# A hybrid decoder step on one core: the sixth tile pair by seven products, four operand sums and four low parts made by GpSimd

## The chip, the core and the metric

The kernel runs on one core of a Trainium2 chip. The core's engines work side by side, each through its own queue: PE (TensorE, the matmuls), DVE (VectorE), ACT (ScalarE), POOL (GpSimd) and SP, which issues DMAs. The metric is the device time of one execution in microseconds. The profile of one execution adds where each engine was busy and what it waited for.

## The reference

One inference step of a one-layer decoder trunk for 512 prompt positions and 8 x 4 sample positions, 544 in all, with a model width of 1024 and an inner width of 4096. A mixer (a recurrent branch and windowed attention) comes first. The change lies in the second half, the convolutional feed-forward block:

```python
def _conv_ffn(h, prev, w_up, conv_w, conv_b, w_down):
    u = h @ w_up                                        # (544, 1024) @ (1024, 8192)
    u, conv_state = _causal_dwconv(u, prev, conv_w, conv_b)   # width 3
    val, gate = jnp.split(u, 2, axis=-1)
    return (jax.nn.gelu(gate, approximate=True) * val) @ w_down, conv_state
```

with `h` the RMS norm of the mixer's output `x`, and the result normed and added to `x`. All of it is in float32.

## The kernel before

**Split matmuls.** Each operand of a matmul is held as a high part (rounded by a copy to a narrower format, on ACT) and a low part (operand minus high part, on DVE). A product is the sum of three matmuls per block of 128 rows: high x high, high x low, low x high. `product` writes one product as 4 blocks x 3 = 12 matmuls with 272 columns; the low part of the weight is read by the third of each three.

**Tile pairs.** The 8192 columns of `w_up` are 64 tiles of 128. Tile p (a value) and tile 32 + p (its gate) form pair p. The 1024 rows of a tile are two halves, and the 544 positions are two halves of 272, so a plain tile takes four products, a plain pair eight. The seven-product form (in the manner of Strassen) treats the pair as a 2 x 2 matrix of weight blocks and the operand as another, and takes seven products, named a11, a12, p2, p3, p1, p4 and a22. It needs four sums of operand blocks (t1, t2, t3, t4, made once, each as two 128x544 tiles with high and low part), and for each pair sums of weight blocks.

**Operands.** `norm_chain(1)` norms the second half of the positions (`h2t`, called `second`), makes the operands b12 and b22 of the plain products, and then, step by step, the sums t2, t3, t1 and t4 from `first` (the tiles `h2f`) and `second`, their high parts (`high`) and low parts (`low`). It is a generator: each `yield x` gives the order back for x ticks, and each product advances the time by half a tick (`slot` calls `round_`). So the place of its instructions among the products is written out by hand. On PE, ACT and DVE instructions run in the order in which the program gives them; POOL's and SP's are ordered by the scheduler of the language.

**The order of products.** Pairs 0 to 3 (`early`) run their first halves while the second half of the positions is still being normed, and then 16 products of their second halves. After these comes the list `plan`: pairs below `PLAIN` as eight plain products (kind "q"), the others by seven (kind "s"), with down halves (kind "dn": 12 matmuls with 256 or 288 columns, one half of the positions of one of eight column tiles of `w_down`, for a group of four pairs) put in behind the products named in `places`. Four down halves go with pairs 4 and 5 together, since the first group is ready only after 12 products of the plan: before, the order is tile 4, tile 36, tile 5 (four products each), three down halves, tile 37, one down half, and then pair 6.

**Weights.** `units` lists the weight halves in the order of their use; a plain unit serves two products, a seven-product unit one. `consumed` counts units, and `ahead` works a fixed number of units ahead of the products: `load` (a DMA of 512 KB into one of five buffers, `raw_up`), `do_high` (ACT, four units ahead), `do_low` (DVE, three ahead), and, for seven-product pairs, `sums`, four and three units ahead of the pair's p2: p3's weight as a sum on DVE into a tile of its own, p1's in place on DVE, and p2's and p4's by two DMAs that add into a second copy of the value tile (`raw_up_s`, a third load of the pair). These two DMAs are issued by POOL, the second after the first has landed.

**Evacuation.** Results of plain products go from PSUM to the tile `u` by copies on ACT (`plain_done`). Results of the seven products are combined: copies `e` on ACT, and additions or subtractions on DVE (`pair`). Then DVE applies the convolution's taps (`tap`), ACT the gelu (`glu` stage 0), DVE the product z (stage 1), and ACT and DVE split z for the down product (stages 2 and 3, fH and fL).

Of the kernel before, what the change touches and what calls it, by code (L numbers as in the profile page):

```python
# [11 lines left out]
F32 = mybir.dt.float32  # L12
F32R = mybir.dt.float32r
AF = mybir.ActivationFunctionType
ALU = mybir.AluOpType
AX = mybir.AxisListType

P = 128
# [40 lines left out]
HP = 150  # L59
NSTART = (1, 0.5)  # L60
EARLY = 4
PLAIN = 6
FB = (0.5,)
LASTS = 6
HELD = 5
TY = 1
TX = 4
DNS = 5
LAST_PLACES = {29: ('p3', 'p1', 'a22'), 30: ('p3', 'p1', 'a22'), 31: ('p1', 'a22')}
FIRST = 5  # L70
ATTN = (8, 10, 12, 14, 16, 18, 20, 22, 24, 26, 29, 32, 35, 38, 40, 42)
SAMPLE = (41, 46)
# [49 lines left out]
def hawk_step(ctx, tc, I, O):  # L122
    nc = tc.nc
    act, dve, pool, pe = nc.scalar, nc.vector, nc.gpsimd, nc.tensor
# [16 lines left out]
    def S(name, dt=F32):  # L141
        return sp.tile([P, SLOT], dt, tag="s", name=name)

    def T(name, dt=F32):
        return tp.tile([P, FLAT + 4], dt, tag="t", name=name)
# [13 lines left out]
    def f32(ap):  # L159
        return ap.bitcast(F32)  # L160
# [4 lines left out]
    def sub(out, a, b):  # L165
        dve.tensor_tensor(out=out, in0=a, in1=b, op=ALU.subtract)  # L166
# [4 lines left out]
    def add(out, a, b):  # L171
        dve.tensor_tensor(out=out, in0=a, in1=b, op=ALU.add)  # L172
# [984 lines left out]
    def total(accs, n, nm):  # L1157

        ps = PX("pst_" + nm)
        for z, acc in enumerate(accs):  # L1160
            mm(ps[:, :n], ones, acc[:, :n], z == 0, z == len(accs) - 1)
        return ps

    def root_table(ps, n, nm):

        y, w = (T(f"{x}_{nm}")[:, :n] for x in ("ry", "rw"))
        act.activation(y, ps[:, :n], AF.Abs_reciprocal_sqrt, scale=1.0 / D, bias=epst)
        act.activation(w, y, AF.Square, scale=1.0 / 32.0)
        return y, w
# [30 lines left out]
    def part_pool(which):  # L1200

        if not parts:
            trans.close()
            parts["e"] = ctx.enter_context(tc.tile_pool(name="parts", bufs=E_BUFS))
            parts["p"] = ctx.enter_context(tc.tile_pool(name="psums", bufs=2))
        return parts[which]
# [6 lines left out]
    def operand(nm, k, j):  # L1213

        if (nm, k // 2) not in B:
            B[nm, k // 2] = [S(f"{nm}{x}{k // 2}", F32R) for x in "HL"]
        return B[nm, k // 2][j][:, (k % 2) * HN:(k % 2 + 1) * HN]

    def operand2(nm, k2, j):

        operand(nm, 2 * k2, j)
        return B[nm, k2][j][:, 0:2 * HN]
# [9 lines left out]
    def norm_chain(a, acc):  # L1232
        lo, hi = HALF2[a]
        n = hi - lo
        with tc.high_priority(offset=HP):
            ps = total([acc], n, f"m{a}")
        yield YS[a]
        with tc.high_priority(offset=HP):
            yw = root_table(ps, n, f"m{a}")
            if a:  # L1240
                yield 0.5
            rep = root_newton(ps, n, *yw)
            acc2 = T(f"accx{a}")
            sq = {}

            def x1_(c):
                return x1[c][:, lo:hi]

            for c in range(0 if a else 8):
                m_ = mt[c][:, lo:hi]  # L1250
                stt(m_, m_, pvn[:, G_POST + c:G_POST + c + 1], rep[:, :n], ALU.mult, ALU.mult)
                pool.tensor_tensor(out=x1_(c), in0=x1_(c), in1=m_, op=ALU.add)
                sq_sum(acc2, x1_(c), n, c == 0, f"x{a}_{c}")
            for g in range(6 if a else 0):
                for c in range(2 * g, 2 * g + 2) if g < 4 else ():
                    m_ = mt[c][:, lo:hi]
                    stt(m_, m_, pvn[:, G_POST + c:G_POST + c + 1], rep[:, :n], ALU.mult, ALU.mult)
                    pool.tensor_tensor(out=x1_(c), in0=x1_(c), in1=m_, op=ALU.add)
                for c in range(2 * g - 3, 2 * g - 1) if 1 <= g < 6 else ():
                    if 0 <= c < 8:  # L1260
                        sq[c] = acc2 if c == 0 else T(f"sq_x{a}_{c}")
                        act.activation(sq[c][:, :n], x1_(c), AF.Square)
                for c in ((), (), (), (), (1, 2, 3), (4, 5, 6, 7))[g]:
                    add(acc2[:, :n], acc2[:, :n], sq[c][:, :n])
                yield 0.5
        yield NORM_TICKS[a]
        with tc.high_priority(offset=HP):
            ps = total([acc2], n, f"f{a}")
        yield YS[a]
        with tc.high_priority(offset=HP):  # L1270
            yw = root_table(ps, n, f"f{a}")
            if a:
                yield 0.5
            rep = root_newton(ps, n, *yw)

            def normed(c, dst):
                stt(dst, x1[c][:, lo:hi], pvn[:, G_FPRE + c:G_FPRE + c + 1], rep[:, :n], ALU.mult, ALU.mult)

            def first(k2):
                return h2f[k2][:, 0:2 * HN]  # L1280

            if a == 0:
                for k2 in range(5):
                    if k2 < 4:
                        for c in (2 * k2, 2 * k2 + 1):
                            normed(c, h2_half0(c))
                        act.activation(operand2(("b11", "b21")[k2 // 2], k2 % 2, 0), first(k2), AF.Copy)
                    if k2:
                        o = [operand2(("b11", "b21")[(k2 - 1) // 2], (k2 - 1) % 2, j) for j in range(2)]
                        sub(o[1], first(k2 - 1), f32(o[0]))  # L1290
                return
            n2 = {}

            def second(k2):
                return n2[k2]

            def high(nm, src):
                for k in range(2):
                    act.activation(operand2(nm, k, 0), src(k), AF.Copy)

            def low(nm, src):
                for k in range(2):
                    sub(operand2(nm, k, 1), src(k), f32(operand2(nm, k, 0)))

            for k2 in range(5):
                if k2 < 4:
                    n2[k2] = npool.tile([P, 2 * HN], F32, name=f"h2t{k2}")
                    for z in range(2):
                        normed(2 * k2 + z, n2[k2][:, z * HN:(z + 1) * HN])
                    act.activation(operand2(("b12", "b22")[k2 // 2], k2 % 2, 0), n2[k2], AF.Copy)  # L1310
                if k2:
                    o = [operand2(("b12", "b22")[(k2 - 1) // 2], (k2 - 1) % 2, j) for j in range(2)]
                    sub(o[1], n2[k2 - 1], f32(o[0]))
                if k2 in (2, 4):
                    yield 0.5
            for c in range(8):
                nc.sync.dma_start(out=x1d[c], in_=x1[c][:, 0:NT])
            t2 = [T(f"t2_{k}")[:, 0:2 * HN] for k in range(2)]
            for k in range(2):
                sub(first(k), first(k), second(k))  # L1320
                stt(t2[k], first(k), -1.0, second(2 + k), ALU.mult, ALU.subtract)
                yield 0.5
            for k in range(2):
                add(first(2 + k), first(2 + k), t2[k])
                yield 0.5
            high("t2", lambda k: t2[k])
            yield 0.5
            low("t2", lambda k: t2[k])
            yield 0.5
            for k in range(2):  # L1330
                sub(second(k), second(k), second(2 + k))
                yield 0.5
            yield TX
            for nm, src in (("t3", second), ("t1", first), ("t4", lambda k: first(2 + k))):
                high(nm, src)
                yield TY
                low(nm, src)
                yield TY

    def out_done(c, acc):  # L1340
# [36 lines left out]
    for p_ in range(EARLY, 32):  # L1377
        if p_ < PLAIN:
            todo_ = [("q", j, u, a) for j in (p_, 32 + p_) for u in range(2) for a in range(2)]
            places = [x for x in todo_ if x[2] == x[3] == 1]  # L1380
        else:
            todo_ = [("s", p_, nm) for nm in (XOF if p_ < 31 else ENDS)]
            places = [x for x in todo_ if x[2] in LAST_PLACES.get(p_, ("a12", "p3", "p1", "a22"))]
        for x in todo_:
# [15 lines left out]
    raws, usplit, used = {}, {}, [0, 0, 0]  # L1400
# [56 lines left out]
    def sums(p_, part):  # L1457
        w = {nm: source(("s", p_, nm)) for nm in ("p1", "p2", "p4", "a22")}
        if part == 0:
            raws["p3", p_] = part_pool("p").tile([P, 4, P], F32, tag="p", name=f"p3_{p_}")  # L1460
            add(raws["p3", p_], w["p2"], w["p1"])
        else:
            add(w["p1"], w["p1"], w["a22"])
            pool.dma_start(out=w["p2"], in_=w["p1"], accum_op=ALU.add)
            pool.dma_start(out=w["p4"], in_=w["p2"], accum_op=ALU.add)  # L1465
# [532 lines left out]
```

## Time and profile before

| what | value |
| --- | --- |
| median of 3 runs | 974.34 us (974.23 to 974.61) |
| the profiled execution | 973.95 us |
| its span in the profile | 972.2 us |
| matmuls on PE | 7634 |
| DVE, ACT, POOL busy | 756.3, 553.9, 167.9 us |

The span runs from the first to the last instruction of the profile; the execution's own time has 1.75 us around it. "Busy" counts the time in which an engine works on an instruction. A row of a timeline gives start, length, engine, line, operation, output <- inputs, shape, and in brackets the idle time of the engine ahead of it and what ended that. A low part of a weight is written `wl_...`, a high part `wh_...`; `pq` is the PSUM tile of plain products, `pux`, `puy`, `puz` those of the seven-product form, `pmdn` that of the down halves.

### The profile page before, as it was taken

The numbers are of one execution on the slowest core, as the hardware profiler recorded it, in microseconds if no ns is written. First come the engines' busy times: TensorE is split into PE (matmuls) and PEld (weight loads), VectorE is DVE, ScalarE is ACT, GpSimd is POOL, SyncE is SP. The second block draws the span as 40 slices with busy tenths as digits, with TensorE's granted clock in tenths as the row PEclk, the third lists the DMA queues.
The fourth block names the chain that finished last, engine by engine and source line by source line (L and its number), as shares of the span: only waits on it lengthen the run. The fifth ranks groups of instructions, "written<-read, shape, count | busy, mean of one in ns | idle before, by whom it ended". The sixth has DMA issues, their size and how long they took to land.

```text
span 972.2 us, 20023 instructions
## 1 busy us (share of the span) xinstructions
PE 963.0 (99%) x7634; PEld 955.2 (98%) x7634; DVE 756.3 (78%) x1599; ACT 553.9 (57%) x1349; POOL 167.9 (17%) x282
## 2 busy tenths in 40 slices
PE   9999999999999999999999999999999999999997
PEld 8999999999999999999999999999999999999996
DVE  5777888857858555599967888787888888888875
ACT  6544443467476425566767665655555555656653
POOL 2242000003406330230010111111011101020024
PEclk9999999999999999999999999999999999999999
DMA  7775535532334547135157575857576766668612
GB/s 229 236 213 180 151 89 147 162 93 87 108 110 128 179 115 189 52 121 186 45 117 182 128 198 123 192 130 181 136 181 157 171 155 156 170 145 219 201 31 92
DMA packets 234203, 143.07 MB, mean 147 GB/s; under 512 B 25012, under 2 KB 218940, under 8 KB 234076
## 3 DMA queue, kind: packets, MB, share of 16 engines
q1 hardware_dynamic: 224300, 120.21, 41.8%
q0 software_dynamic: 9696, 19.42, 11.8%
q10 hardware_dynamic: 112, 2.17, 0.6%
q8 instruction: 60, 0.98, 0.4%
q14 instruction: 35, 0.29, 0.1%
HBM read 115.59 MB, written 15.17 MB: 134 GB/s over the span
## 4 chain that ended last, share of the span: by engine, by line
PE 94%; DVE 3%; ACT 1%; issue 0%; DMA 0%; POOL 0%; SPq 0%; DVEq 0%; ACTq 0%; POOLq 0%
PE pmin L163 20%; PE pmdn L163 19%; PE pux L1527 16%; PE puy L1527 8%; PE pq L1527 6%; PE pmlo L163 5%; PE pmao L163 5%; PE pmout L163 4%; PE puz L1527 4%; PE pg L163 1%; PE pvp L163 1%; PE psc L163 1%; PE ptok L163 1%; DVE wl_e L166 0%; DMA pt<-pd 0%
## 5 line engine op out<-in xcount | busy, mean ns | idle before, releaser
L163 PE MATMUL pmin<-hH,wh_in 128*128 128x256 f32 (+1 forms) x568 | 164.0, 291 | 0.0
L163 PE MATMUL pmin<-hL,wh_in 128*128 128x256 f32 (+1 forms) x568 | 162.4, 288 | 0.0
L163 PE MATMUL pmin<-hH,wl_in 128*128 128x256 f32 (+1 forms) x568 | 159.1, 288 | 0.0
L163 PE MATMUL pmdn<-fH,wh_dn 128*128 128x256 f32 (+1 forms) x448 | 129.2, 288 | 0.0
L163 PE MATMUL pmdn<-fH,wl_dn 128*128 128x256 f32 (+1 forms) x448 | 129.0, 288 | 0.0
L163 PE MATMUL pmdn<-fL,wh_dn 128*128 128x256 f32 (+1 forms) x448 | 128.9, 288 | 0.0
L163 PEld LDWEIGHTS pmin<-hH,wh_in 128*128 128x128 f32 x568 | 107.2, 189 | 1.2 <-issue 1.0
L163 PEld LDWEIGHTS pmin<-hL,wh_in 128*128 128x128 f32 x568 | 107.2, 189 | 0.1
L163 PEld LDWEIGHTS pmin<-hH,wl_in 128*128 128x128 f32 x568 | 104.7, 188 | 0.2 <-issue 0.2
L175 DVE SCALAR_TENSOR_TENSOR uc<-u,fv,uc 128x560 f32<-128x560 f32 x128 | 102.0, 797 | 1.7 <-ACT uc L1558 1.1
L163 PEld LDWEIGHTS pmdn<-fH,wl_dn 128*128 128x128 f32 x448 | 84.4, 188 | 0.0
L163 PEld LDWEIGHTS pmdn<-fL,wh_dn 128*128 128x128 f32 x448 | 84.3, 188 | 0.1
L163 PEld LDWEIGHTS pmdn<-fH,wh_dn 128*128 128x128 f32 x448 | 84.2, 188 | 0.1
L1655 ACT COPY u<-pux 128x272 f32<-128x272 f32 x52 | 20.1, 387 | 86.0 <-PE pux L1527 86.0
L166 DVE TENSOR_TENSOR u<-puy,u 128x240 f32<-128x240 f32 (+2 forms) x78 | 24.6, 344 | 49.6 <-PE puy L1527 32.5
L172 DVE TENSOR_TENSOR ft<-ft,pmdn 128x256 f32<-128x256 f32 (+1 forms) x104 | 45.1, 434 | 16.7 <-PE pmdn L163 16.7
L281 ACT ACTIVATE wh_in<-raw_in 128x512 fp32r<-128x512 f32 x70 | 42.2, 625 | 19.0 <-issue 10.6
L288 DVE TENSOR_TENSOR wl_in<-raw_in,wh_in 128x512 fp32r<-128x512 f32 x70 | 47.8, 693 | 1.0 <-ACT wh_in L281 1.0
L1558 ACT ACTIVATE uc<-u,fv 128x560 f32<-128x560 f32 x64 | 48.2, 755 | 0.0
L779 ACT ACTIVATE s<-s,st 128x256 f32<-128x256 f32 (+1 forms) x32 | 15.2, 475 | 53.0 <-DVE st L776 42.5
L166 DVE TENSOR_TENSOR wl_dn<-raw_dn,wh_dn 128x512 fp32r<-128x512 f32 x56 | 38.3, 685 | 3.6 <-ACT wh_dn L1476 3.6
L1465 POOL DMA_DIRECT2D raw_up_s<-raw_up_s x26 | 22.4, 861 | 93.2 <-DMA raw_up_s<-raw_up__11237 5.5
(743 smaller groups left out, 3374.9 us busy)
## 6 DMA issues: line engine op xcount, KB each, us to landing
raw_in<-in_w_in_dram SPq DMA_DIRECT2D x35, 512.0 KB
raw_dn<-in_w_down_dram SPq DMA_DIRECT2D x56, 256.0 KB
raw_up_s<-in_w_up_dram SPq DMA_DIRECT2D x25, 512.0 KB
raw_up_s<-raw_up_s POOLq DMA_DIRECT2D x26, 256.0 KB, 4.3
raw_ao<-in_w_attn_o_dram SPq DMA_DIRECT2D x8, 512.0 KB
raw_lo<-in_w_lru_o_dram SPq DMA_DIRECT2D x8, 512.0 KB
raw_out<-in_w_out_dram SPq DMA_DIRECT2D x8, 512.0 KB
pd<-pb SPq DMA_DIRECT2D x12, 256.0 KB
```

Source lines behind the costliest of these rows:

```text
L163: pe.matmul(out, l, r, start=start, stop=stop)
L166: dve.tensor_tensor(out=out, in0=a, in1=b, op=ALU.subtract)
L172: dve.tensor_tensor(out=out, in0=a, in1=b, op=ALU.add)
L175: dve.scalar_tensor_tensor(out=out, in0=a, scalar=s_, in1=b, op0=op0, op1=op1)
L281: act.activation(hl[0], raw, AF.Copy)
L288: (eng or dve).tensor_tensor(out=hl[1], in0=raw, in1=f32(hl[0]), op=ALU.subtract)
L779: act.activation(s3[:, j, :], s3[:, j, :], AF.Exp, bias=ng[:, j:j + 1], accum_out=sm[:, j:j + 1])
L1465: pool.dma_start(out=w["p4"], in_=w["p2"], accum_op=ALU.add)
L1527: pe.matmul(ps[:, :HN], w, x, start=start and k == 0 and i == 0, stop=stop and k == 3 and i == 2, skip_group_check=True)
L1558: act.activation(yt[j][:, 0:FLATU], u[:, 0:FLATU], AF.Copy, scale=fv[:, j:j + 1])
L1655: act.copy(e[nm_], z)
```

## The change

Pair 5 moves from eight plain products to the seven-product form. In the plan, tiles 4 and 36 stay as they are; then come a11, a12, p2, p3, two down halves, p1, one down half, p4, a22, one down half, and then pair 6. Everything behind that has the order of before. Pair 5 thus takes a third load, two weight sums on DVE and two accumulating DMAs, and its sum for p3 lies in one of the general slots (`S`).

In `norm_chain(1)`, the sums of t3 (`second(k)`, two tiles) and the last step of t4 (`first(2 + k)`, two tiles) are made by POOL in place of DVE, all four at one place ahead of t2's high parts. The low parts of t3 and t4 (two tiles each) are made by POOL as well; those of t2 and t1 stay on DVE. The order is now t2, t3, t4, t1 with shorter waits between (`TX` 2 in place of 4, and four half ticks fewer).

```diff
-PLAIN = 6
+PLAIN = 5
...
-TX = 4
+TX = 2
 DNS = 5
-LAST_PLACES = {29: ('p3', 'p1', 'a22'), 30: ('p3', 'p1', 'a22'), 31: ('p1', 'a22')}
+LAST_PLACES = {5: ('p1', 'a22'), 29: ('p3', 'p1', 'a22'), 30: ('p3', 'p1', 'a22'), 31: ('p1', 'a22')}
...
-            def low(nm, src):
+            def low(nm, src, eng=dve):
                 for k in range(2):
-                    sub(operand2(nm, k, 1), src(k), f32(operand2(nm, k, 0)))
+                    eng.tensor_tensor(out=operand2(nm, k, 1), in0=src(k), in1=f32(operand2(nm, k, 0)), op=ALU.subtract)
...
             for k in range(2):
-                add(first(2 + k), first(2 + k), t2[k])
-                yield 0.5
+                pool.tensor_tensor(out=second(k), in0=second(k), in1=second(2 + k), op=ALU.subtract)
+            for k in range(2):
+                pool.tensor_tensor(out=first(2 + k), in0=first(2 + k), in1=t2[k], op=ALU.add)
+            yield 0.5
             high("t2", lambda k: t2[k])
             yield 0.5
             low("t2", lambda k: t2[k])
-            yield 0.5
-            for k in range(2):
-                sub(second(k), second(k), second(2 + k))
-                yield 0.5
             yield TX
-            for nm, src in (("t3", second), ("t1", first), ("t4", lambda k: first(2 + k))):
+            for nm, src, eng in (("t3", second, pool), ("t4", lambda k: first(2 + k), pool), ("t1", first, dve)):
                 high(nm, src)
                 yield TY
-                low(nm, src)
+                low(nm, src, eng)
                 yield TY
...
         if part == 0:
-            raws["p3", p_] = part_pool("p").tile([P, 4, P], F32, tag="p", name=f"p3_{p_}")
+            if p_ == PLAIN:
+                raws["p3", p_] = S(f"p3_{p_}")[:, 0:512].rearrange("p (k n) -> p k n", k=4)
+            else:
+                raws["p3", p_] = part_pool("p").tile([P, 4, P], F32, tag="p", name=f"p3_{p_}")
             add(raws["p3", p_], w["p2"], w["p1"])
```

## The prediction, made before the result was known

> **What bounds the kernel now.** I read the page first, then busy time by stage around the edit.
>
> ```profile
> span 972.2 us, 20023 instructions
> PE 963.0 (99%) x7634; PEld 955.2 (98%) x7634; DVE 756.3 (78%) x1599; ACT 553.9 (57%) x1349; POOL 167.9 (17%) x282
> ...
> 448.00:460.00 12.00, 12.00 (x97) 12.00 (x97) 11.11 (x23) 8.26 (x25) 0.00 (x0) 1.00 0.40 122
> 460.00:472.00 12.00, 12.00 (x98) 12.00 (x97) 10.17 (x20) 10.33 (x33) 0.00 (x0) 1.00 0.07 25
> 472.00:484.00 12.00, 12.00 (x98) 12.00 (x97) 11.71 (x22) 9.68 (x26) 0.00 (x0) 1.00 0.22 65
> 484.00:496.00 12.00, 12.00 (x98) 12.00 (x98) 8.23 (x16) 6.43 (x17) 1.81 (x2) 1.00 0.60 146
> ```
>
> In the stage rows the columns after the window are its length and the busy time of PE, PEld, DVE, ACT and POOL, then clock, DMA share and GB/s. PE is busy 12.00 of 12.00 us in each, at clock 1.00: from the early pairs on, the end is set by the number of matmuls. DVE is the second: 11.11, 10.17 and 11.71 of 12 before 484, but only 8.23 behind it. POOL does nothing from 448 to 484. So the saving is to be had on PE, and the danger is that DVE falls behind in exactly this stretch.
>
> Next the chain of work that ended last, in order of time, for what a product costs and when each is due.
>
> ```profile
> 436.32 49.67 PE pq L1527 x396
> 485.99 4.43 PE pmdn L163 x36
> ...
> 498.03 1.52 PE pux L1527 x12
> ```
>
> 396 matmuls are 33 products of 12, so one takes 49.67 / 33 = 1.505 us; a product of the seven-product form (pux) takes 1.52. By the plan, the last four of the 33 are tile 5, the first of pair 5, so the pair starts at 485.99 - 4 x 1.505 = 479.97. Its other tile, 37, follows the three down halves.
>
> **What PE saves.** Pair 5 goes from eight products to seven, with four down halves before and after: one product less, **-1.5 us**. PE had no gap here, so no more than this can be won; it is 0.15% of the time. About 0.2% (1.95 us) is what a measurement of this kernel can tell from no change.
>
> **When things fall due.** In the new order pair 5 starts at the same 479.97, and its first four products are a11, a12, p2, p3 (479.97, 481.48, 482.98, 484.49), then the first down half at 485.99, as before. The difference: before, one split weight served two products (a = 0 and 1), so a new one was due every 3.0 us; now each product has its own, due every 1.5 us. The low part of a weight is read by the third matmul of its product, 0.25 us into it. The lows are made on DVE in a fixed order, so DVE's timeline decides:
>
> ```profile
> 448.36 0.72 DVE L172 TENSOR_TENSOR h2f<-h2f,t 128x544 f32<-128x544 f32 x1
> ...
> 454.88 1.35 DVE L166 TENSOR_TENSOR h2t<-h2t,h2t 128x544 f32<-128x544 f32 x2
> ...
> 458.63 0.91 DVE L175 SCALAR_TENSOR_TENSOR z<-uc,fv,uc 128x512 f32<-128x512 f32 x2 [0.82 <-ACT uc L1569]
> ...
> 464.12 0.92 DVE L175 SCALAR_TENSOR_TENSOR z<-uc,fv,uc 128x512 f32<-128x512 f32 x2 [0.82 <-ACT uc L1569]
> ...
> 472.00 1.36 DVE L166 TENSOR_TENSOR t3L<-h2t,t3H 128x544 fp32r<-128x544 f32 x2
> ...
> 475.47 0.69 DVE L166 TENSOR_TENSOR wl_q<-raw_up__6115,wh_q 128x512 fp32r<-128x512 f32 x1
> ...
> 477.21 1.35 DVE L166 TENSOR_TENSOR t1L<-h2f,t1H 128x544 fp32r<-128x544 f32 x2
> 478.48 0.69 DVE L166 TENSOR_TENSOR wl_q<-raw_up__6115,wh_q 128x512 fp32r<-128x512 f32 x1
> ...
> 481.27 0.69 DVE L166 TENSOR_TENSOR wl_dn<-raw_dn,wh_dn 128x512 fp32r<-128x512 f32 x1
> ...
> 481.88 0.68 DVE L172 TENSOR_TENSOR p<-raw_up_s,raw_up__6410 128x512 f32<-128x512 f32 x1
> ```
>
> The columns are start and length. DVE is in one line of work: its only idle times are the 0.82 us before a z, where it waits for ACT's gelu of the tile it has just tapped. The three lows at 475.47, 478.48 and 481.27 are the ones that a11, a12 and p2 take over: the code issues the split of the same unit number after the same product.
>
> **What DVE loses and gains, without any contention.** Ahead of the low of p2, it loses two adds (0.72 each, like 448.36), two subtractions (1.35) and t3's low (1.36): -4.15. It gains pair 5's two weight sums, issued right at the start of this stretch (0.68 each, like tile 6's at 481.88): +1.36. Net -2.8. Its end was 481.27 + 0.69 = 481.96, so 479.2; it is due at 482.98 + 0.25 = 483.23: **margin 4.0 us**. a11's low has t1's low (1.35) ahead of it as well: 476.16 - 1.4 = 474.8, due 480.22, margin 5.4. a12: 479.17 - 2.8 = 476.4, due 481.73, margin 5.3. p2 decides. t4's low goes to POOL too, but lies behind all of these.
>
> **What the eight POOL instructions cost DVE.** No 128x544 POOL instruction stands in the trace; the nearest are 128x568, seen here in order of time with what DVE did meanwhile:
>
> ```profile
> 237.28 0.75 DVE L175 SCALAR_TENSOR_TENSOR lt<-lt,th 128x568 f32<-128x568 f32 x1 [0.66 <-POOL lt L1005]
> ...
> 240.08 1.42 POOL L1014 TENSOR_TENSOR xc<-xc,lt 128x568 f32<-128x568 f32 x1
> 240.15 1.96 DVE L175 SCALAR_TENSOR_TENSOR lt<-lt,th 128x568 f32<-128x568 f32 x1 [0.70 <-POOL lt L1005]
> ...
> 429.20 0.89 DVE L175 SCALAR_TENSOR_TENSOR mt<-mt,pvn,pst_m 128x272 f32<-128x272 f32 x2
> 430.02 1.18 DVE L166 TENSOR_TENSOR wl_e<-raw_up__5779,wh_e 128x512 fp32r<-128x512 f32 x1
> ```
>
> The same DVE instruction takes 0.75 us alone and 1.96 with a POOL instruction just ahead of it: 1.21 more, nearly the POOL instruction's whole 1.42. At 430.02 a weight's low takes 1.18 instead of 0.69 beside POOL's narrower 128x272 work, while the pair at 429.20, whose second operand lies in PSUM, isn't held. So a DVE instruction with two SBUF tiles stands still while POOL works. Every long DVE row quoted from 448.36 on has two SBUF tiles. Scaled to 544 elements the block is 1.21 x 544 / 568 = 1.16 us; eight make 9.3. All eight are issued between about 447 and 470 by the yields, ahead of pair 5's lows. The sums meet a DVE without idle time and cost in full; the lows of t3 and t4 come where two of the 0.82 waits lie, and I let those hide 1.6. That leaves **7.7 us**. Lower end: 0.49 each (430.02), 3.9; upper end: 1.21 each and nothing hidden, 9.7. I take 7.7 because the rows at 240 are the nearest in width and operands.
>
> [...]
>
> **The sum.** 7.7 us against a margin of 4.0: PE waits 3.7 for the low parts of a11, a12 and p2 together. -1.5 + 3.7 = **+2.2 us**. The profiled execution took 973.95 (span 972.2 and 1.75 around it): 976.15. The median of the runs is 974.34, 0.4 higher, and gives 976.5; I say 976.3. Ends: 3.9 gives no wait, -1.5; 9.7 gives 5.7 - 1.5 = +4.2.
>
> **What I cost at nothing, and its cover.** Pair 5's third load (512 KB) takes the place on SP's queue where tile 6's stood:
>
> ```profile
> 438.75 2.69 SPq L1440 DMA_DIRECT2D raw_up__6340<-in_w_up_dram  x1
> ...
> 485.64 0.94 POOL L1464 DMA_DIRECT2D raw_up_s<-raw_up__6410  x1 [53.81 <-DVE raw_up__6410 L172]
> 489.26 0.87 POOL L1465 DMA_DIRECT2D raw_up_s<-raw_up_s  x1 [2.68 <-DMA raw_up_s<-raw_up__6410]
> ```
>
> Tile 6's own loads move behind it, into a stretch with a DMA share of 0.07. The two accumulating transfers queue on POOL: the second waits for the first, so from 485.64 to 489.26 + 0.87 the queue is held 4.5 us, and t3's and t4's lows may sit behind it. That is covered: t3 is due at 484.5, some 20 us after it can be made; t4 at 493.5; t2's operands stay early, due at 483; t1's low goes to t3's old place at 472.00, due at 489. Were that cover gone, POOL's wait would be PE's. Pair 5's evacuations (four small DVE instructions and three copies on ACT in place of copies on ACT alone) lie behind 481, where DVE is busy 8.23 of 12; without that room they'd cost at most their own 1 to 2 us.
>
> **Rivals.**
> [...]
> 2. *The weight sum waits for its load*: the first sum of pair 5 now stands at the head of DVE's line near 448, and its third load is issued near 439 to 441, when DMA is crowded. If it lands 3 to 5 us late, everything behind stands still, less what POOL uses of it: +4 to +7, 978 to 981. Against it: the load in that place found a free path (DMA share falls to 0.40 after 448).
> 3. *The change does not do what it says*: the seven products could cost as much as eight. 1.52 against 1.505 excludes it; the count of matmuls must fall by 12.
>
> **Chances.** Forecast (PE waits 2 to 5.7 us, 974.4 to 978.5): 0.57. Rival 1 and the little waits up to 2 us: 0.30. Rival 2 or worse: 0.10. Faster by more than PE can give, through measurement alone: 0.03. Of the forecast, two thirds lie above +1.95, so slower is 0.38 + 0.10 = 0.48, same 0.19 + 0.30 = 0.49, faster 0.03. The likeliest case's own range is 974.4 to 978.5; with rival 1 in it, 972.4 to 978.5 leaves out 0.13.
>
> **What the next profile would show.** Right: PE x7622; POOL with eight 128x544 rows of 1.2 to 2 us between 447 and 470; DVE rows of 1.8 to 2 us beside them instead of 0.7 to 0.8; idle time of PE some 2.5 to 6 us between 480 and 486, ended by DVE's lows of pair 5. Wrong: PE at 12.00 in those windows and DVE rows of unchanged length (rival 1), or a DVE wait ended by a DMA near 448 (rival 2). What would make me wrong in size is the 1.6 hidden and the 4.0 margin, each good to about 1.5 us.

## The result and the profile after

The changed kernel takes 979.99 us (median of 6 runs, 979.88 to 980.17), the kernel before in the same comparison 974.37: ratio 1.0058, interval 1.0045 to 1.0071, so 5.6 us slower. The forecast was 976.3, the range ended at 978.5. The profiled execution has a span of 977.9 against 972.2.

The page of the kernel after, its first lines:

```profile
span 977.9 us, 20035 instructions
PE 964.9 (99%) x7622; PEld 956.2 (98%) x7622; DVE 764.6 (78%) x1600; ACT 556.5 (57%) x1351; POOL 182.1 (19%) x292
```

PE issues 12 matmuls less, as it should, yet is busy 1.9 us longer. The same four stages as before the change show where (columns as in the prediction):

```profile
448.00:460.00 12.00, 12.00 (x98) 12.00 (x97) 11.93 (x17) 7.80 (x24) 6.91 (x5) 1.00 0.19 43
460.00:472.00 12.00, 12.00 (x98) 12.00 (x98) 10.18 (x13) 6.36 (x18) 6.59 (x5) 1.00 0.55 148
472.00:484.00 12.00, 8.81 (x69) 8.38 (x67) 10.99 (x19) 8.94 (x27) 0.15 (x1) 1.00 0.01 2
484.00:496.00 12.00, 10.76 (x72) 10.39 (x73) 11.30 (x21) 9.93 (x28) 0.86 (x1) 0.86 0.29 86
```

Three things are new: in the first window DVE is as busy as a window allows (11.93) with 17 instructions where it had 23, beside 6.91 us of POOL; PE loses 3.2 us in the third window; and in the fourth it loses 1.2 us more and its granted clock is 0.86 on average. From 496 to 900 PE is busy throughout at clock 1.00, as before.

**DVE beside POOL.** The timeline of the kernel after, DVE and POOL in order of time:

```profile
446.82 1.76 POOL L1324 TENSOR_TENSOR h2t<-h2t,h2t 128x544 f32<-128x544 f32 x1 [14.67 <-ACT wh_q L1477]
447.28 1.89 DVE L166 TENSOR_TENSOR h2f<-h2f,h2t 128x544 f32<-128x544 f32 x1
448.54 1.85 POOL L1326 TENSOR_TENSOR h2f<-h2f,t 128x544 f32<-128x544 f32 x1
449.20 1.77 DVE L175 SCALAR_TENSOR_TENSOR t<-h2f,h2t 128x544 f32<-128x544 f32 x1
450.35 1.85 POOL L1324 TENSOR_TENSOR h2t<-h2t,h2t 128x544 f32<-128x544 f32 x1
450.90 1.84 DVE L172 TENSOR_TENSOR p<-raw_up_s,raw_up__6159 128x512 f32<-128x512 f32 x1
452.16 1.81 POOL L1326 TENSOR_TENSOR h2f<-h2f,t 128x544 f32<-128x544 f32 x1
452.67 1.85 DVE L166 TENSOR_TENSOR wl_q<-raw_up__6014,wh_q 128x512 fp32r<-128x512 f32 x1
...
462.24 3.96 DVE L175 SCALAR_TENSOR_TENSOR z<-uc,fv,uc 128x512 f32<-128x512 f32 x2 [0.89 <-ACT uc L1570]
462.50 2.97 POOL L1303 TENSOR_TENSOR t3L<-h2t,t3H 128x544 fp32r<-128x544 f32 x2
...
468.31 2.61 DVE L175 SCALAR_TENSOR_TENSOR uc<-u,fv,uc 128x560 f32<-128x560 f32 x2
468.96 3.19 POOL L1303 TENSOR_TENSOR t4L<-h2f,t4H 128x544 fp32r<-128x544 f32 x2 [3.48 <-ACT t4H L1299]
...
471.76 1.10 DVE L175 SCALAR_TENSOR_TENSOR z<-uc,fv,uc 128x512 f32<-128x512 f32 x2 [0.82 <-ACT uc L1570]
```

Read the first eight as a zip: the rows overlap, but each DVE row ends some 0.6 us, about its own length, after a POOL row has ended (448.58 and 449.17, 450.39 and 450.97), and every row takes 1.8 us: the engines take turns. The four DVE rows sum to 7.35; the same four kinds took 0.72, 0.73, 0.68 and 0.69 before, 2.82. That is 4.5 us lost for four sums. The z at 462.24 lost 3.96 - 0.91 = 3.05, the uc at 468.31 0.98 (1.63 without POOL), the z at 471.76 0.19. Together **8.75 us** for eight instructions.

The two pairs of lows cost different amounts. t3's pair began at 462.50, just after DVE's wait for gelu had ended, and the first instruction of the z (3.80 of the 3.96 us) stood through both of its rows: 1.5 us each, nothing hidden. Why both ran ahead of it, where the sums took turns with DVE, no run shows. t4's pair cost 0.98 + 0.19 = 1.17, 0.6 us each: its second row ran mostly while DVE waited for gelu in any case (the 0.82 us before the z at 471.76). So about half of t4's pair was hidden. The sum at 450.90 shows no wait for its load.

**What PE waited for.** PE has three waits from 470 to 496. Their rows, with DVE's lows for a11 and for p2, ACT's gelu and ACT's copy `e` beside them, in order of time:

```profile
480.61 0.39 PE L1528 MATMUL pux<-b11H,wh_s_a 128*128 128x272 f32 x1 [0.31 <-ACT wh_s_a L1477]
...
483.28 0.69 DVE L166 TENSOR_TENSOR wl_s_a<-raw_up__6115,wh_s_a 128x512 fp32r<-128x512 f32 x1
483.39 0.76 ACT L1570 ACTIVATE uc<-uc,fv 128x560 f32<-128x560 f32 x1 [2.56 <-DVE u L1535]
484.02 0.40 PE L1528 MATMUL pux<-b11H,wl_s_a 128*128 128x272 f32 x1 [2.89 <-DVE wl_s_a L166]
...
486.05 0.73 DVE L166 TENSOR_TENSOR fL<-z,fH 128x544 fp32r<-128x544 f32 x1 [0.34 <-ACT fH L1578]
488.27 0.69 DVE L166 TENSOR_TENSOR wl_s_p<-raw_up_s,wh_s_p 128x512 fp32r<-128x512 f32 x1
...
489.19 0.37 ACT L1656 COPY e<-pux 128x272 f32<-128x272 f32 x1
489.61 0.40 PE L1528 MATMUL pux<-t2H,wh_s_p 128*128 128x272 f32 x1 [1.22 <-ACT e L1656]
```

a11 waits 0.31 us for its high part, made on ACT, and then 2.89 for its low part, as forecast. p2 waits for something that the prediction did not have: p2 is added into the same PSUM tile (`pux`) as a11, so it can't begin until ACT has copied a11's result out, and that copy ran at 489.19, in its turn in ACT's queue. That queue was late itself: ACT had waited 2.56 us for DVE's taps ahead of the gelu at 483.39, and from there it worked almost without a break up to the copy. So DVE's delay reaches PE by two ways, the low parts and ACT's queue. DVE's low for p2 ended at 488.96, and it is read by p2's third matmul. Without the copy, p2 would have been held as long as if it had started at about 488.7; the copy adds the 0.9 us from there to 489.61.

**The clock.** Busy time and granted clock of the kernel after, microsecond by microsecond:

```profile
485.00:486.00 1.00, 1.00 (x8) 0.95 (x7) 0.70 (x2) 0.97 (x6) 0.00 (x0) 0.70 0.00 0
486.00:487.00 1.00, 1.00 (x6) 1.00 (x6) 0.95 (x2) 1.00 (x3) 0.00 (x0) 0.50 0.08 24
487.00:488.00 1.00, 1.00 (x7) 1.00 (x5) 0.96 (x2) 1.00 (x4) 0.00 (x0) 0.50 0.64 173
488.00:489.00 1.00, 0.39 (x2) 0.07 (x1) 1.00 (x4) 0.97 (x6) 0.00 (x0) 0.59 1.05 314
```

About 1.4 us after PE resumed from its 2.89 us of idleness the granted clock fell to 0.50, and a12 ran at half speed. The lost clock adds up to 0.30 + 0.50 + 0.50 + 0.41 = 1.71 us.

The chain of the kernel after gives the sum:

```profile
436.63 37.65 PE pq L1528 x300
...
489.61 1.79 PE pux L1528 x12
...
492.90 3.02 PE pmdn L163 x24
```

The stage began at 436.63 (before: 436.32) and the first down half stands at 492.90 (before: 485.99): 6.9 us later. Of these 0.3 was there when the stage began, 4.4 is idle time (0.31 + 2.89 + 1.22), and the other 2.2 is the half clock and the restarts (p2's twelve matmuls take 1.79, not 1.52). The product that was saved comes behind it, -1.5: 5.4, and 0.3 more by the end of the span.

### The profile page after: what moved, and what is told of

Its sections match the earlier page's. It is cut to its first block, busy times and chain, and to the rows that moved or that the text cites. A ratio compares the mean times of both kernels' runs of the same rounds, so it can differ in the third digit from the quotient of the medians.

```text
span 977.9 us, 20035 instructions
## 1 busy us (share of the span) xinstructions
PE 964.9 (99%) x7622; PEld 956.2 (98%) x7622; DVE 764.6 (78%) x1600; ACT 556.5 (57%) x1351; POOL 182.1 (19%) x292
## 4 chain that ended last, share of the span: by engine, by line
PE 91%; DVE 4%; ACT 2%; issue 1%; DMA 0%; POOL 0%; SPq 0%; DVEq 0%; ACTq 0%; POOLq 0%
PE pmin L163 20%; PE pmdn L163 17%; PE pux L1528 16%; PE puy L1528 8%; PE pmlo L163 5%; PE pmao L163 5%; PE pmout L163 4%; PE puz L1528 4%; PE pq L1528 4%; PE pg L163 1%; PE pvp L163 1%; PE psc L163 1%; PE ptok L163 1%; DVE uc L175 1%; DVE wl_e L166 0%
```

## The experiments

The theory after this reading, A: GpSimd's eight instructions stop DVE for their own length, and this is what the kernel lost; the rival, B: it is the closer due times of seven products (and the new order of the sums) that DVE can't meet, with or without GpSimd. Four kernels take the parts one by one, three more test what these left open. Each is compared with the kernel before on the same chip: 974.30 us for e1 to e4, 974.45 for e5 to e7.

| kernel | median us | ratio, interval |
| --- | --- | --- |
| e1: after, all eight on DVE | 977.43 | 1.0033, 1.0019 to 1.0046 |
| e2: before, pair 5 by seven products | 974.55 | 1.0002, 0.9993 to 1.0012 |
| e3: after, pair 5 by eight products | 976.74 | 1.0026, 1.0016 to 1.0036 |
| e4: before, eight extra GpSimd subtractions | 979.36 | 1.0054, 1.0039 to 1.0069 |
| e5: before, eight GpSimd memsets | 973.82 | 0.9993, 0.9983 to 1.0002 |
| e6: e2, t4's parts six products later | 973.47 | 0.9989, 0.9980 to 0.9998 |
| e7: after, the old order of the sums | 979.45 | 1.0051, 1.0037 to 1.0065 |

**e1, the kernel after without GpSimd's share.** The four sums and four lows go back to DVE, in the new order and at the new times:

```diff
-            for nm, src, eng in (("t3", second, pool), ("t4", lambda k: first(2 + k), pool), ("t1", first, dve)):
+            for nm, src, eng in (("t3", second, dve), ("t4", lambda k: first(2 + k), dve), ("t1", first, dve)):
```

(and `pool.tensor_tensor` in the two sums to `dve.tensor_tensor`).

> The changed kernel with all eight sums and low parts back on VectorE, at the same places in the program; pair 5 still by seven products. Theory A (a GpSimd instruction stops VectorE for about 1.15 us, and that lateness reaches TensorE): VectorE does 5.6 us of own work where it stood still for 8.8, so p2's low part ends near 484.7, some 1.4 us late; with a little more for the PSUM bank, about 974.8 us (974 to 976). Theory B (the seven-product form needs its weights too early, whoever makes the operands): nothing is won, 979 to 980 us.

977.43 (five runs, 976.17 to 978.58): 2.6 us less than after, but not the 974.8 expected (974 to 976). PE has one wait, and behind it the clock drops again (PE waits of e1; then its windows):

```profile
PE pux L1528 <- ACT e L1656: 2.3, 1, 2.3
```

```profile
486.00:487.00 1.00, 1.00 (x7) 1.00 (x7) 1.00 (x4) 1.00 (x3) 0.00 (x0) 0.64 0.00 0
487.00:488.00 1.00, 1.00 (x6) 1.00 (x6) 0.96 (x2) 0.48 (x1) 0.00 (x0) 0.50 0.27 81
488.00:489.00 1.00, 1.00 (x6) 1.00 (x6) 1.00 (x3) 0.40 (x2) 0.00 (x0) 0.50 0.61 181
489.00:490.00 1.00, 1.00 (x8) 1.00 (x7) 1.00 (x2) 1.00 (x2) 0.00 (x0) 0.65 0.00 0
```

Here PE had work all the while, so the half clock cost its whole 0.36 + 0.50 + 0.50 + 0.35 = 1.71 us: -1.5 + 2.3 + 1.7 + 0.3 for the restart and 0.3 for the stage's later begin (436.62) is 3.1, as measured. So GpSimd is not the only cause. In the new order DVE has t4's and t1's lows ahead of the taps and of p2's low, and ACT's queue stands behind a gelu that waits for the taps (timeline of e1, ACT and DVE):

```profile
479.63 0.76 ACT L1570 ACTIVATE uc<-uc,fv 128x560 f32<-128x560 f32 x1 [2.57 <-DVE u L1535]
...
484.50 0.69 DVE L166 TENSOR_TENSOR wl_s_p<-raw_up_s,wh_s_p 128x512 fp32r<-128x512 f32 x1
```

The wait that ends last is the one for ACT's copy of a11, but p2's low is late as well. It ended at 485.19, and PE had been free since 483.52: without the copy p2 would have been held as if it had started at about 484.9. So 1.4 of the 2.3 us are DVE's lateness, as expected, and the copy adds 0.9.

**e2, the seven products alone.** The kernel before with `PLAIN = 5`, the down halves' places and the slot for p3's sum, and nothing else:

```diff
-PLAIN = 6
+PLAIN = 5
```

> The kernel before with pair 5 by seven products and nothing else: operand sums, low parts and their times as before. Theory A: only pair 5's two weight sums (1.36 us) are added ahead of the lows; the low of p3, behind t4's, is about 0.6 us late, so -1.5 + 0.6 to 1: about 973.6 us (972.8 to 974.4). Theory B: the weights are late by the tighter spacing alone, 977 to 980 us.

974.55, no gain where a whole product was to be had, and just above what was expected (972.8 to 974.4). The page's count of matmuls is 7622, so the product is gone. The waits of PE and ACT's rows in front of the copy, both of e2:

```profile
PE pux L1530 <- ACT e L1658: 1.1, 1, 1.1
```

```profile
480.49 1.19 ACT L1299 ACTIVATE t4H<-h2f 128x544 fp32r<-128x544 f32 x2
...
483.68 0.36 ACT L1658 COPY e<-pux 128x272 f32<-128x272 f32 x1
```

PE waits for no low part. The saving goes into a wait of 1.1 us for the copy `e`, which stands in ACT's queue behind, among others, the two high parts of t4 (1.19 us of solid work for the two together).

**e3, GpSimd's share alone.** The kernel after with `PLAIN = 6`: pair 5 by eight products, the operand chain as changed.

> The kernel before with the GpSimd part of the change alone: pair 5 stays plain, eight instructions on GpSimd, order and times of the changed kernel. Theory A: VectorE loses 4.15 us of work and t1's low (1.35) moves ahead, but it stands still 8.8 us; tile 5's first low ends near 482.2, due 480.2, so TensorE waits 2 us and a little more for what is late behind it: 976.4 to 978 us. Theory B: nothing to wait for, 974.4 us.

976.74, inside what was expected: GpSimd's share, with the new order of the sums, costs 2.4 us even where no weight is due earlier. PE has one wait, and the granted clock behind it stays at 1.00 (PE waits of e3, then a window):

```profile
PE pq L1528 <- DVE wl_q L166: 1.6, 1, 1.6
```

```profile
482.00:484.00 2.00, 1.80 (x14) 1.81 (x15) 1.66 (x4) 1.97 (x8) 0.00 (x0) 1.00 0.00 0
```

**e4, the block by itself.** The kernel before with eight extra subtractions of 128x544 on GpSimd into a spare tile that nothing reads:

```diff
+            def extra(n):
+                for _ in range(n):
+                    pool.tensor_tensor(out=spare, in0=f32(operand2("b12", 0, 0)), in1=f32(operand2("b12", 1, 0)), op=ALU.subtract)
+            extra(4)
...
+            yield 1
+            extra(2)
+            yield 2
+            extra(2)
+            yield 1
```

> The kernel before, with nothing moved, and eight more 128x544 subtractions on GpSimd into a spare tile that nobody reads, at the places of the change (four, two, two). Theory A: each stops VectorE's next instruction by 1.0 to 1.2 us, with no relief for it: tile 5's first low ends 8 to 9 us later, near 484.5, due 480.2: TensorE waits 4 to 6 us, 978.5 to 980.5 us. If GpSimd's work costs VectorE nothing: 974.4 us, and rows of unchanged length.

979.36, as expected: work that feeds nothing costs 5.1 us. All eight ran in one block, since POOL's order is the scheduler's (timeline of e4, POOL and one of DVE's rows beside it):

```profile
442.32 14.01 POOL L1327 TENSOR_TENSOR spare<-b12H,b12H 128x544 f32<-128x544 f32 x8 [10.29 <-issue]
...
447.81 1.87 DVE L166 TENSOR_TENSOR h2f<-h2f,h2t 128x544 f32<-128x544 f32 x1
```

The row is like those of the kernel after (there 0.72 without POOL). The waits of PE in e4:

```profile
PE pq L1538 <- DVE wl_q L166: 1.9, 1, 1.9
PE pq L1538 <- DVE b22L L166: 1.2, 2, 0.8
```

After the 1.9 us the granted clock is 0.90, 0.50, 0.50, 0.50, 0.89 in the five microseconds from 484: again 1.71 us lost. 1.9 + 1.2 + 1.7 and the restarts make the 5.1.

**e5, the same with memsets.** `pool.memset(spare, 0.0)` in place of e4's subtraction: GpSimd writes the tile but reads nothing.

> The kernel before plus eight memsets of a 128x544 spare tile on POOL, in the same places as e4's eight extra subtractions; nothing reads the tile. It tells apart what stops DVE. Theory A (POOL's work stops DVE only through POOL instructions that read two SBUF tiles): DVE's 128x544 and 128x512 rows beside the memsets stay at 0.7 us, PE has no idle time, 974.4 us (974.0 to 974.8). Theory B (any POOL instruction that touches SBUF stops DVE for its whole length): the rows beside them take 0.7 us plus the memset's length; with eight memsets of 0.5 to 1.5 us, DVE loses 4 to 10 us, and the time goes the way of e4, 976 to 979.5.

973.82, as fast as before (the interval holds 1), and a little under what was expected (974.0 to 974.8). The scheduler put the eight memsets even earlier, and the low part of a weight, an instruction with two inputs in SBUF, lies beside them at its usual length (timeline of e5, POOL and DVE):

```profile
432.30 4.84 POOL L1327 MEMSET spare<- 128x544 f32 x8
433.41 0.69 DVE L166 TENSOR_TENSOR wl_e<-raw_up__5777,wh_e 128x512 fp32r<-128x512 f32 x1
```

Two more lows beside the later memsets take 0.68 each. So GpSimd at work did not by itself hold DVE here (0.69 beside memsets that only write); in e4, beside subtractions that read two tiles, the row above took 1.87 for 0.72. The place differs from e4's, so the time of e5 alone proves less than this row does.

**e6, e2 with ACT's queue cleared.** One line: t4's high and low parts, which are due last, come six products later.

```diff
             for nm, src in (("t3", second), ("t1", first), ("t4", lambda k: first(2 + k))):
+                if nm == "t4":
+                    yield 3
                 high(nm, src)
```

> The seven products alone (all eight operand instructions on DVE, the order and times of before), but t4's high and low parts issued 3 ticks, that is six products, later. In the kernel with the seven products alone PE waited 1.1 us ahead of p2 for ACT's copy of a11's result out of the PSUM bank that p2 uses too, and t4's two high parts (1.10 us each) stood ahead of that copy in ACT's queue. Theory A (the copy is late because of this queue): with t4's high parts behind it, the copy ends by about 482.8, PE has no idle time or under 0.3 us between 478 and 492, and the time falls by one product: 972.7 to 973.6, likeliest 973.1. Theory B (the copy waits for something else, such as gelu's operand from DVE): the wait stays near 1 us and the time near 974.5.

973.47: 1.0 us under before and the fastest of all, just outside what the interval allows for no change. Since e5, which has nothing to gain, came out 0.6 under in the same comparison, the time alone proves little. (The expectation's 1.10 us for each of t4's high parts is the length of the two together.) The trace is clear (timeline of e6, ACT and PE, then pieces of its chain):

```profile
483.33 0.36 ACT L1660 COPY e<-pux 128x272 f32<-128x272 f32 x1
483.75 0.40 PE L1532 MATMUL pux<-t2H,wh_s_p 128*128 128x272 f32 x1
```

```profile
437.06 43.64 PE pq L1532 x348
...
497.52 1.50 PE pux L1532 x12
```

No wait is left in the stage. From its first product to pair 6's a11 it takes 497.52 - 437.06 = 60.46 us; before, 498.03 - 436.32 = 61.71. So 1.25 of the 1.5 us are gained. The stage itself began 0.7 us later than before, which no edit explains (below).

**e7, the kernel after with the old order and times of the sums** (t3, t1, t4; `TX = 4`, the four half ticks back), GpSimd's share kept.

> The kernel after, with POOL's eight instructions kept, but the order and times of before for the operand chain (t3, t1, t4; the last low two products' time later). It completes a square: e1 has the new order without POOL's work, the seven products alone have neither, the kernel after has both. Theory A (POOL's work delays DVE's lows for pair 5 by 7 to 9 us, and the order only adds to it): DVE's low for p2 ends near 486 to 488, PE idles about 3 us ahead of a11 to p2 and then runs at half the clock for some 3 us: 977 to 979. Theory B (the new order is the main cause, POOL's share is hidden by the later t4): under 976.

979.45, above what was expected (977 to 979) and hardly better than after (979.99). PE waits 0.8 us for a12's low, 2.1 for the copy of a11 and 0.7 for p2's low, and then loses 1.71 us of clock. The lows of t4 on GpSimd now run just when p2's low is due (timeline of e7, POOL and DVE):

```profile
483.60 3.53 POOL L1303 TENSOR_TENSOR t4L<-h2f,t4H 128x544 fp32r<-128x544 f32 x2 [8.24 <-ACT t4H L1299]
...
483.32 2.59 DVE L175 SCALAR_TENSOR_TENSOR uc<-u,fv,uc 128x560 f32<-128x560 f32 x2
485.84 1.83 DVE L166 TENSOR_TENSOR wl_s_p<-raw_up_s,wh_s_p 128x512 fp32r<-128x512 f32 x1
```

That completes a square (us against before): old order without GpSimd +0.25 (e2), new order without +3.1 (e1), old order with +5.0 (e7), both +5.6 (after). With GpSimd's share the order hardly matters; without it, the new order alone loses 3. From e2, GpSimd's share alone costs 4.8, the order alone 2.9, both 5.4: the two overlap. Theory A carries the larger part; B holds for the order, not for the spacing of the weights: in e2 and e6 PE waits for no low part.

## Why the prediction was wrong

- **What PE saves, -1.5: right.** 7622 matmuls; e6 gains 1.25 of it. Rival 3 is refuted.
- **Due times: right.** PE was free for a11 at 480.30 (479.97 forecast, and 0.3 for the stage's later begin) and waited from there, the first 0.31 us for the high part on ACT, for which the prediction had no due time.
- **DVE's own work, -2.8 ahead of p2's low: right as far as it can be seen.** Its one added term, two weight sums at +1.36, reads in e2 as the low for p2 ending at 483.18 in place of 481.96, +1.2. It is a little less than the lengths say because DVE's rows overlap (t3's lows at 472.00 take 1.36, and the next row starts at 473.27); by starts the net is -2.65, not -2.8.
- **The block, 1.16 each, 9.3 in all: right in kind and nearly in size.** The rows give 8.75: 1.13 for each sum, 1.5 for each low of t3, 0.6 for each low of t4. e4 shows that it costs the kernel time by itself, e3 that it does so together with the new order. That DVE stands still "while POOL works" is too wide: it did beside instructions of GpSimd that read two tiles (1.87 us for 0.72, e4) and did not beside memsets (0.69, e5). A block nearer 0.49, which is rival 1 in the chances, is refuted: the rows give 8.75 / 8 = 1.09 on average. No run shows rival 1's 972.4, GpSimd's share for nothing and the whole product won; the fastest, e6, has no share of GpSimd and takes 973.47.
- **"I let those hide 1.6": wrong in size.** This is the first step that failed. It took 0.8 off each pair of lows. t4's pair hid more than that (1.17 lost, not 2 x 1.16 = 2.32), t3's pair nothing (3.05 lost): next in POOL's queue after the accumulating DMA at 461.93, it began when the wait for gelu was over. The four lows cost 4.2 where the forecast had 2 x 2.32 - 1.6 = 3.0. DVE's low for p2 ended at 488.96. The forecast's own terms put it at 479.2 + 7.7 = 486.9, and with the stage's 0.3 at 487.2. Of the missing 1.8 us, 1.05 is the block (8.75, not 7.7), 0.4 is further waiting of DVE (0.34 of it for ACT's fH at 486.05), 0.15 the overlap of the rows, and the rest is not accounted for. So the delay was not 7.7 but 488.96 - 479.2 - 0.3 = 9.5, close to the upper end that the prediction had put at 9.7 and +4.2. By itself this would have given +4.0, 978.3, which the forecast's range still holds.
- **"What I cost at nothing": wrong for pair 5's evacuations.** This is the second, and the one that carries the time past the range. They were costed as time on DVE and ACT, and there was room for them; but ACT's copy of a11 is also what releases PSUM tile x for p2, and p2 comes only one product (a12) after a11. In e2 that alone takes 1.1 of the 1.5 us, in e1 0.9 of the 2.3; e6 shows that in e2 it was ACT's queue. In the kernel after it decides p2's start by the last 0.9 us (489.61 against some 488.7), in a queue that DVE's late taps had held up. The step's own bound, 1 to 2 us without cover, would have held e2's and after's.
- **The sum's 3.7 us of waiting by PE: too small**, 4.4 measured, **and what follows an idle PE was missing**: the half clock. In e1, e4 and e7 it cost 1.7 us each. In the kernel after it slowed a12, but p2 had to wait for the copy in any case, so it is not a term to be added there.
- **The other covers held.** Rival 2 is refuted by the row at 450.90; GpSimd's lows of t3, behind two DMAs on POOL's queue, started at 462.50 and ended 19 us ahead of a first use near 484.5; what the queue changed is where they met DVE.
- **A slip in the chances:** a wait of 2 us gives 974.8, not the 974.4 that stands beside it. Nothing hangs on it.

With the measured terms the working gives -1.5, + 9.5 - 4.0 = 5.5 for DVE, + 0.9 for the copy, + 0.3 for the restart: 5.2, and 0.3 from the stage's later begin: 5.5 of the 5.6 measured. The 0.3 of the stage's begin stays open. It lies between 436.32 (before) and 437.06 (e6) in the profiles, ahead of everything that the edits touch; what moves it was not tried.

## What to carry to other kernels

Work given to an engine with idle time is free only if its rows don't hold those of another: look for rows where both engines read SBUF tiles at once, take the longer length for every such row (1.8 us for 0.7 beside the four sums here), and count on a gap only where the row is sure to fall into it. When products become closer, ask for each PSUM tile who empties it and what stands ahead of that copy in its engine's queue, not only when the operands are ready. Follow a delay of one engine into every queue that waits for it: here DVE's reached PE through ACT as well. A wait of PE can have a price of its own beyond its length: 1.71 us of lost clock behind waits of 1.9 us and more here, none behind 1.1 and 1.6. Here one line that moves late-due work behind an evacuation (e6) was worth more than eight instructions moved to another engine.

## What the runs showed of the hardware

- **The same spell behind four idle times of PE.** Waits of 1.9 (e4), 2.3 (e1) and 2.89 us (after), and the 2.1 and 0.7 us that lie together in e7, were each followed by a spell at granted clock 0.50 that adds up to 1.71 us of lost clock, 3.42 us at half speed, in all four; after waits of 1.1 (e2) and 1.6 us (e3) the clock stayed at 1.00. The spell begins 0.5 to 1.4 us after PE has resumed from the long wait (e7: 0.2 us after the short one). In a stretch as long as the spell (3.4 us) just ahead of it PE had stood 1.87 (e4), 2.03 (after), 2.31 (e1) and 2.68 us (e7). In e2 and e3 no such stretch holds more than 1.12 and 1.56. No run lies between 1.56 and 1.87, and none shows what sets the spell's length.
- **GpSimd pays as well.** Beside DVE its 128x544 rows take 1.76 to 1.85 us in the zip of the kernel after, while the pair of t3's lows at 462.50 takes 2.97 for two, about 1.5 each, beside the z that stands still. e4's eight take 14.01 / 8 = 1.75 each beside DVE's rows.
